# Two-layer SSD and MLA step in split fp32: norms of a series issued at once or a unit later, weights scaled on ScalarE, five PSUM banks at the scan's end

## Chip, cores and metric

One core of a Trainium2 chip runs the whole kernel. The metric is the device time of one execution in microseconds; lower is better. Engines are named as in the profile: PE (TensorE, with PEld for its weight loads), DVE (VectorE), ACT (ScalarE), POOL (GpSimd) and SP (SyncE, which here only issues DMAs).

## The reference

One inference step of a trunk of two layers over a prompt of 1024 tokens and a sample of 32 tokens, width 1024, all in fp32. Layer 0 mixes tokens by a Mamba-2 scan, layer 1 by latent attention, and each layer ends with a gated product of per-layer embeddings (`ple`). Cut to what matters here:

```python
def ple(h, p, up_w, norm_w, gate_w):
    g = sigmoid(rmsnorm(h, norm_w) @ gate_w)
    return (p @ up_w) * g
# each layer
hn = rmsnorm(h, ln_w[i]);  h = h + mixer(hn);  h = h + ple(h, p[i], ...)
# the mixer of layer 1
q_a, kv_a, k_r, gate = split(hn @ in_w, [384, 640, 672])
q      = (rmsnorm(q_a) @ q_b_w).reshape(T, 16, 96)
q_nope = rmsnorm(q[..., :64]);  q_rope = apply_rope(rmsnorm(q[..., 64:]), cos, sin)
lat    = rmsnorm(kv_a);         k_rope = apply_rope(rmsnorm(k_r), cos, sin)
kv     = (lat @ kv_b_w).reshape(T, 16, 128);  k_nope = rmsnorm(kv[..., :64]);  v = kv[..., 64:]
o      = chunk_causal_attention(q_nope, q_rope, k_nope, k_rope, v) * silu(gate)
out    = o @ out_w
```

The sample attends over a cache of 1024 past latents as well. Outputs are both hidden streams, the conv and scan states, and the new latents and rotary keys.

## The kernel before

Activations lie transposed: 128 features on the partitions, tokens along the free dimension. Prompt and sample are put together as 1056 tokens in two halves of 528. A product in fp32 is made of three products in the faster fp32r form: activation and weight are split into a high part (rounded to fp32r) and a low part (the rest), and `gemm` (line 245 is its matmul) adds up wh·ah, wh·al and wl·ah over the blocks k of 128 features. `load_weight` gets one weight block: a DMA on SP into `wraw` (two buffers), where a scale is given the multiply by it (one gain per input feature, so one number per partition and k), the copy to `wh` on ACT (L204) and the difference `wl` on POOL (L205). A block of 128 outputs over 8 k's on one half of 528 tokens is 48 matmuls of 264 columns; here it is called a product, and its result a pair of banks `pg` or `psi`, of which there are three.

The phases, with their stretch of the profiled execution in us:

- 0 to 781, `phase_ssd`: 8 groups of the scan. At the last group's end the products p @ up_w of layer 0 (`up_product`, results `upe`, stored to `u_d`) run while `finish` normalises the last group.
- 781 to 973, `phase_out`, the output product `pso` of layer 0.
- 973 to 1069, `phase_ple`: for m in 0 to 7 and two halves, a gate product `pg`, then t = pg·r (DVE, L806), tanh (ACT, L188), u·(1 + tanh) (DVE, L189), plus the residual `hr` that POOL adds up (DVE, L810). Then `emit` stores the new h to DRAM, splits it into `yhl` (ACT L259, DVE L260), squares it (ACT L702) and adds the square to `acc` (POOL L703). The weights gateW are scaled by the gain of the norm; the norm's r is one factor per token, made by `norm_r`: a matmul n of the squares with ones (L710), ln and exp.
- 1069 to 1247, `phase_mla_in`: with the scaled weights miW and krW two latent blocks, the rotary key, three blocks of q_a and eight gate blocks, each on two halves (`mblock`). r1[hf], the norm of the layer's input, is made at the first product of its half, directly behind that product's matmuls.
- 1247 to 1398, `phase_sample`: the attention of 32 tokens, interleaved with up products of layer 1 (`pup`) and with the first steps of the prompt, `Prompt.prep(0)` and `rope_block(0)`.
- 1398 to 1790, `phase_prompt`: 8 pairs of heads; `values` makes the products `psv` from the value weights vW, `fill` puts operands into `qk`, `row_max` the scores s (L1343) for the maxima, `head` the transposed scores `st` and the output o.
- 1790 to 1889 and 1889 to 1985: `phase_out` and `phase_ple` of layer 1.

`Prompt.prep` and `rope_block` are generators: each step makes a product for a group of heads, issues the norm of the product before it (`norm_now`, matmul `hn`, L936) and puts its own into `self.norms`; the last norm of a series follows when the generator is resumed after its last step. `rope_block` then swaps halves of the rotary rows by eight small DMAs on SP (L1211, L1212), loads cosines and sines (L1217, L1218) and combines them.

Within a phase the order of instructions on each engine is not the order of the code: a scheduler with a simulated timeline (`schedule_with_timeline_sim=True`) sets it when the program is built, by its own estimates, and each engine then runs its list in order. So an edit can shift instructions that it doesn't touch.

Of the kernel before, what the change touches and what calls it, by code (L numbers as in the profile page):

```python
# [10 lines left out]
F32 = mybir.dt.float32  # L11
F32R = mybir.dt.float32r
AF = mybir.ActivationFunctionType
ALU = mybir.AluOpType
# [3 lines left out]
P = 128  # L18
# [154 lines left out]
def bc_last(ap, n):  # L173
    return ap.unsqueeze(len(ap.shape)).to_broadcast(list(ap.shape) + [n])
# [17 lines left out]
def load_weight(c, src, nk, m, scale=None, eng_h=None, wp=None, wr=None):  # L192
    nc = c.nc
    wp = wp or c.wp
    raw = (wr or wp).tile([P, nk, m], F32, tag="wraw", name="wraw")
    nc.sync.dma_start(raw, src)
    if scale is not None:
        nc.gpsimd.tensor_tensor(raw, raw, bc_last(scale, m), op=ALU.mult)
    wh = wp.tile([P, nk, m], F32R, tag="wh", name="wh", bufs=c.whb)
    wl = wp.tile([P, nk, m], F32R, tag="wl", name="wl", bufs=c.whb)  # L200
    if eng_h:
        eng_h.tensor_copy(wh, raw)
    else:
        nc.scalar.activation(wh, raw, AF.Copy)  # L204
    nc.gpsimd.tensor_tensor(wl, raw, wh.bitcast(F32), op=ALU.subtract)  # L205
    return wh, wl


def load_stacked(c, src, nk, m, scale=None, eng_h=None):

    nc = c.nc
    raw = c.wp.tile([P, nk, m], F32, tag="wraw", name="wraw")
    nc.sync.dma_start(raw, src)
    if scale is not None:
        nc.gpsimd.tensor_tensor(raw, raw, bc_last(scale, m), op=ALU.mult)
    w = c.wp.tile([P, nk, 2 * m], F32R, tag="wh", name="whl", bufs=c.whb)
    wh, wl = w[:, :, :m], w[:, :, m:]
    if eng_h:
        eng_h.tensor_copy(wh, raw)
    else:  # L220
        nc.scalar.activation(wh, raw, AF.Copy)
    nc.gpsimd.tensor_tensor(wl, raw, wh.bitcast(F32), op=ALU.subtract)
    return w
# [39 lines left out]
def pvc(c, name, i=0, n=1, rows=P):  # L263
    o, _ = PV[name]
    return c.pv[:rows, o + i : o + i + n]


def up_product(c, i, piece, raw, tiles, ps_tile, evac, nb=1):

    nc, I = c.nc, c.I  # L270
    o, n = piece
    acts = []
    for k in range(2):
        x = raw()[:, :n]
        nc.sync.dma_start(x, I[f"pT{i}"][:, k, o : o + n])
        h, l = tiles()[:, :n], tiles()[:, :n]
        split(c, h, l, x)
        acts.append((h, l))
    yield
    na = -(-n // 512)  # L280
    w_ = n // na
    for m in range(8):
        b = m % nb
        if b == 0:
            ws = load_weight(c, I[f"upW{i}"][m // 4][:, 2 * (m % 4) : 2 * (m % 4 + nb)], 2 * nb, P)
        w = [x[:, 2 * b : 2 * b + 2] for x in ws]
        u = evac()
        for a in range(na):
            ps = ps_tile()
            gemm(c, ps[:, :w_], w, acts, slice(w_ * a, w_ * a + w_))  # L290
            if nb > 1 and a % 2:
                nc.vector.tensor_copy(u[:, w_ * a : w_ * a + w_], ps[:, :w_])
            else:
                nc.scalar.activation(u[:, w_ * a : w_ * a + w_], ps[:, :w_], AF.Copy)
        c.store(c.u_d[i][m][:, o : o + n], u[:, :n])
        yield
# [8 lines left out]
def phase_ssd(c, ctx):  # L305
    nc, tc, I, O = c.nc, c.tc, c.I, c.O
# [3 lines left out]
    mm = es.enter_context(tc.tile_pool(name="ps_mm", bufs=3, space=bass.MemoryType.PSUM))  # L310
    pc = es.enter_context(tc.tile_pool(name="ps_c", bufs=1, space=bass.MemoryType.PSUM))
# [334 lines left out]
    for g in range(G):  # L646
        scan_group(g, Ss[g])
        if g + 1 < G:
            bc_blocks(g + 1)
        if g:  # L650
            gate(g - 1, 0, Ss[g - 1])
            gate(g - 1, 1, Ss[g - 1])
        if g + 1 < G:
            x_block(g + 1, 0)
        else:
            gate(g, 0, Ss[g])
        if g:
            finish(g - 1, Ss[g - 1])
        if g + 1 < G:
            x_block(g + 1, 1)  # L660
            if g == 0:

                for p in steps:
                    tc.add_manual_dep(p, c.product.ins.name, mybir.DependencyInfo(
                        mybir.DependencyClass.NoSync, mybir.DependencyReason.DATA), reason="late operand")
        else:
            up = up_product(c, 0, (0, T), lambda: kp.tile([P, T1], F32, tag="cx", name="upr", bufs=6),
                            lambda: kp.tile([P, 3 + T1], F32R, tag="raw", name="upx", bufs=RAWB),
                            lambda: mm.tile([P, 512], F32, tag="mm", name="mm"),
                            lambda: kp.tile([P, T1], F32, tag="cx", name="upe", bufs=6), 4)  # L670
            next(up)
            gate(g, 1, Ss[g])
            finish(g, Ss[g])
# [13 lines left out]
def gemm2(c, ps, w, acts, first=True, last=True):  # L687

    n = len(acts)
    for k in range(n):  # L690
        for a in range(2):
            gemm(c, ps[:, a, :264], [x[:, k : k + 1] for x in w], acts[k : k + 1], slice(264 * a, 264 * a + 264),
                 first=first and k == 0, last=last and k == n - 1)
# [120 lines left out]
def phase_mla_in(c, h1s, r1, tmp, yt, mt, st, latents_done):  # L814
# [3 lines left out]
    def wt(name, tag):  # L818
        return yt.tile([P, 528], F32, tag=tag, name=name, bufs=RAWY if tag == "yraw" else 2)

    def mblock(wsrc, m, evac):
        w = (load_stacked if m < P else load_weight)(c, wsrc, 8, m, scale=pvc(c, "lnw1", 0, 8))
        for hf in range(2):
            ps = mm2(c, "psi")
            if m < P:
                for a in range(2):
                    gemm_stacked(c, ps[:, a, :264], w, h1s[hf], slice(264 * a, 264 * a + 264), m)
            else:
                gemm2(c, ps, w, h1s[hf])
            if callable(r1[hf]):  # L830
                r1[hf] = r1[hf]()
            evac(hf, ps[:, :, :264])

    def latent(nblk, wofs, n, wname, done):
        raws = [[None] * nblk for _ in range(2)]
# [352 lines left out]
class Prompt:  # L1188
# [7 lines left out]
    def rope_block(self, g):  # L1196
        c, nc, I = self.c, self.c.nc, self.c.I
        w = load_weight(c, I["qrW"][g], 3, P)
        rope = c.pre.tile([P, 2, 1024], F32, tag="rope", name="rope")
        sw, fq = rope[:, 0], rope[:, 1]  # L1200
        for a in range(2):
            cols = slice(512 * a, 512 * a + 512)
            ps = c.ps.tile([P, 512], F32, tag=self.tag, name="psr", bufs=2)
            gemm(c, ps, w, self.st.qan, cols)
            self.norm_now()
            self.norms.append((fq[:, cols], head_sq(c, ps, fq[:, cols]), pvc(c, "qr"), (c.bd32, 32)))
            yield
        self.norm_now()
        for h in range(4):
            lo, hi = slice(32 * h, 32 * h + 16), slice(32 * h + 16, 32 * h + 32)  # L1210
            nc.sync.dma_start(sw[lo], fq[hi])  # L1211
            nc.sync.dma_start(sw[hi], fq[lo])  # L1212
        for a in range(2):
            cols = slice(512 * a, 512 * a + 512)
            wc = c.pre.tile([P, 512], F32, tag="hsh", name="wcos", bufs=2)
            ws = c.pre.tile([P, 512], F32, tag="hsl", name="wsin", bufs=2)
            nc.sync.dma_start(wc, I["cosT"][:, cols])  # L1217
            nc.sync.dma_start(ws, I["sinT"][:, cols])  # L1218
            nc.vector.tensor_tensor(fq[:, cols], fq[:, cols], wc, op=ALU.mult)
            nc.vector.tensor_tensor(sw[:, cols], sw[:, cols], ws, op=ALU.mult)  # L1220
            nc.vector.tensor_tensor(fq[:, cols], fq[:, cols], sw[:, cols], op=ALU.add)
        h, l = sw.bitcast(F32R), fq.bitcast(F32R)
        nc.scalar.activation(h, fq, AF.Copy)
        nc.vector.tensor_tensor(l, fq, sw, op=ALU.subtract)
        self.rope = rope.bitcast(F32R)

    def prep(self, p):

        c, I = self.c, self.c.I
        self.x[p] = out = []  # L1230
        for wsrc, nk, acts, wn in ((I["qnW"][p], 3, self.st.qan, "qn"), (I["kW"][p], 2, self.st.latp, "kn")):
            w = load_weight(c, wsrc, nk, P)
            for a in range(2):
                ps = c.ps.tile([P, 512], F32, tag=self.tag, name="psqk", bufs=2)
                gemm(c, ps, w, acts, slice(512 * a, 512 * a + 512))
                x = c.pre.tile([P, 512], F32, tag="hx", name="hx", bufs=5)
                self.norm_now()
                self.norms.append((x, head_sq(c, ps, x), pvc(c, wn), (c.bd64, 64)))
                out.append(x)
                yield  # L1240
        self.norm_now()

    def norm_now(self):

# [366 lines left out]
```

## Time and profile before

| | before |
|---|---|
| median of 3 runs | 1989.59 us (1989.28 to 1992.05) |
| the profiled execution | 1990.86 us, span 1989.1 us |
| granted TensorE clock, mean | 0.990 |
| PE busy | 1922.0 us (97%), 12763 matmuls |
| DVE, ACT, POOL busy | 1217.8, 1064.9, 996.0 us |
| DMA | 204.26 MB, mean 103 GB/s |

The span runs from the first to the last instruction of the profiled execution; the device time holds 1.8 us more. Busy times overlap between engines. A row of waits reads: engine, its operation and line, what it waited for; total us, times, longest. A row of the timeline reads: start, duration, engine, line, operation, output<-inputs, and in brackets the idle time just ahead on that engine with what ended it. SPq is the queue of SP, where DMAs are issued.

### The profile page before, as it was taken

What the parts mean: (1) busy time and instruction counts of PE and PEld (TensorE: products, weight loads), DVE (VectorE), ACT (ScalarE), POOL (GpSimd) and SP (SyncE); (2) the same over time, 40 slices, a digit from 0 to 9 for tenths busy, and PEclk for the clock granted to TensorE, in tenths of its full rate; (3) what the DMA queues carried; (4) which work ended last, traced back from release to release, by engine and by line L of the source; (5) the groups of instructions that cost most, each with busy time, mean ns of one, the idle gap of its engine ahead of it and who ended that gap; (6) DMA issues with size and microseconds to landing.
All of it is one profiled execution on the core that took longest, in us unless ns stands there. A gap on an engine that the chain in (4) does not pass through costs nothing. (4 is left out here: it accounts for less than half of the span.)

```text
span 1989.1 us, 32537 instructions
## 1 busy us (share of the span) xinstructions
PE 1922.0 (97%) x12763; PEld 1768.4 (89%) x12763; DVE 1217.8 (61%) x1533; ACT 1064.9 (54%) x1990; POOL 996.0 (50%) x828
## 2 busy tenths in 40 slices
PE   8999999999999999999998999998899999999999
PEld 7998999999999998999998999677678777779999
DVE  7979684755757485452376543544677777755544
ACT  5445645455555546342434331777587878754331
POOL 5643434344442545545676452324466666635772
PEclk9999999999999999999999999999899999999999
DMA  4143442524333436563333221424412222316442
GB/s 142 54 97 83 102 105 76 105 74 96 91 79 86 102 100 246 167 201 109 97 115 118 73 73 71 153 83 127 98 47 72 68 54 66 112 38 200 124 130 72
DMA packets 110730, 204.26 MB, mean 103 GB/s; under 512 B 18224, under 2 KB 60720, under 8 KB 110448
## 3 DMA queue, kind: packets, MB, share of 16 engines
q1 hardware_dynamic: 105328, 193.04, 33.4%
q0 software_dynamic: 2944, 7.04, 1.8%
q8 instruction: 100, 1.64, 0.3%
q10 hardware_dynamic: 2304, 2.10, 0.3%
q14 instruction: 54, 0.44, 0.1%
HBM read 156.81 MB, written 38.83 MB: 98 GB/s over the span
## 5 line engine op out<-in xcount | busy, mean ns | idle before, releaser
L205 POOL TENSOR_TENSOR wl<-wraw,wh 128x1024 fp32r<-128x1024 f32 (+3 forms) x183 | 373.1, 2040 | 374.0 <-ACT wh L204 350.5
L245 PE MATMUL mm<-hh,wl 128*128 128x384 f32 (+1 forms) x1136 | 371.5, 327 | 0.0
L245 PE MATMUL mm<-hh,wh 128*128 128x384 f32 (+1 forms) x1136 | 371.1, 327 | 0.0
L245 PE MATMUL mm<-hl,wh 128*128 128x384 f32 (+1 forms) x1136 | 368.9, 325 | 0.0
L204 ACT ACTIVATE wh<-wraw 128x1024 fp32r<-128x1024 f32 (+3 forms) x181 | 157.1, 869 | 240.7 <-PE pso L245 96.5
L245 PE MATMUL pso<-yhl,wh 128*128 128x264 f32 x1536 | 282.9, 286 | 0.9 <-DVE hf L765 0.4
L245 PEld LDWEIGHTS pso<-yhl,wh 128*128 128x128 f32 x1536 | 238.9, 189 | 1.5 <-ACT yhl L259 1.0
L245 PE MATMUL pso<-yhl,wl 128*128 128x264 f32 x768 | 218.9, 285 | 3.6 <-POOL wl L205 3.6
L245 PEld LDWEIGHTS mm<-hh,wh 128*128 128x128 f32 x1136 | 213.5, 188 | 3.5 <-issue 3.2
L245 PEld LDWEIGHTS mm<-hl,wh 128*128 128x128 f32 x1136 | 213.8, 188 | 0.8 <-issue 0.2
L245 PEld LDWEIGHTS mm<-hh,wl 128*128 128x128 f32 x1136 | 213.5, 188 | 0.9 <-issue 0.2
L503 DVE SCALAR_TENSOR_TENSOR cx<-raw,pv,cx 128x1060 f32<-128x1060 f32 x96 | 144.7, 1511 | 44.0 <-ACT cx L501 43.4
L566 ACT ACTIVATE ex<-ex,tokT 128x128 f32<-128x128 f32 (+1 forms) x288 | 87.2, 380 | 136.3 <-DMA ex<-acs_d 128.5
L245 PE MATMUL psi<-yhl,wh 128*128 128x264 f32 x832 | 156.3, 289 | 1.6 <-ACT yhl L259 1.2
L1363 PE MATMUL st<-qk 128*128 128x512 f32 (+2 forms) x576 | 149.0, 370 | 4.6 <-ACT pf L1369 3.3
L245 PEld LDWEIGHTS pso<-yhl,wl 128*128 128x128 f32 x768 | 145.6, 190 | 4.6 <-POOL wl L205 4.6
L245 PE MATMUL pg<-hH,wl 128*128 128x264 f32 x512 | 145.5, 284 | 1.3 <-POOL wl L205 1.3
L245 PE MATMUL pg<-hH,wh 128*128 128x264 f32 x512 | 146.1, 285 | 0.0
L245 PE MATMUL pg<-hL,wh 128*128 128x264 f32 x512 | 145.7, 285 | 0.0
L579 POOL TENSOR_TENSOR hm<-hT,cd_all 128x256 f32<-128x256 f32 x64 | 53.6, 838 | 162.1 <-DVE hT L581 97.0
L245 PEld LDWEIGHTS psi<-yhl,wh 128*128 128x128 f32 x832 | 131.5, 192 | 2.9 <-ACT yhl L259 1.4
L1345 DVE TENSOR_REDUCE mx<-s 128x1 f32<-128x128 f32 (+2 forms) x192 | 101.8, 550 | 50.6 <-PE s L1343 49.4
(547 smaller groups left out, 4638.3 us busy)
## 6 DMA issues: line engine op xcount, KB each, us to landing
wraw<-in_inW SPq DMA_DIRECT2D x48, 512.0 KB, 3.5
ex<-acs_d SPq DMA_DIRECT2D x32, 512.0 KB, 5.5
wraw<-in_outW SPq DMA_DIRECT2D x32, 512.0 KB, 3.8
yraw<-y_d SPq DMA_DIRECT2D x32, 264.0 KB, 4.6
u<-u_d SPq DMA_DIRECT2D x32, 264.0 KB, 2.9
eb<-ea_d SPq DMA_DIRECT2D x64, 128.0 KB, 3.8
y_d<-y SPq DMA_DIRECT2D x16, 512.0 KB, 2.8
wraw<-in_gateW SPq DMA_DIRECT2D x16, 512.0 KB, 3.5
```

The lines of the kernel that those rows point to most:

```text
L204: nc.scalar.activation(wh, raw, AF.Copy)
L205: nc.gpsimd.tensor_tensor(wl, raw, wh.bitcast(F32), op=ALU.subtract)
L245: p = c.nc.tensor.matmul(ps, ww[:, k, :m], aa, start=first and k == 0 and i == 0, stop=last and k == n - 1 and i == 2)
L503: nc.vector.scalar_tensor_tensor(xh, raw[:, k : k + T1], pvc(c, "cw", 4 * b + k), xh, op0=ALU.mult, op1=ALU.add)
L566: nc.scalar.activation(e_, e_, AF.Relu, scale=-1.0, bias=tok(32)[:, i, h : h + 1])
L579: nc.gpsimd.tensor_tensor(hm.rearrange("p (h q) -> p h q", q=64), hT.rearrange("p (h q) -> p h q", q=64), bc_last(cd_all[:, hs, ch], 64), ...
L1345: nc.vector.tensor_reduce(mx[:, col : col + 1], ps[:, : (w if b else 128)], axis=AX.X, op=ALU.max)
L1363: nc.tensor.matmul(ps[:, :n], a_[:, ks], b_[:, q], start=t == 0, stop=t == 2)
```

## The change

Four edits.

- `load_weight` and `load_stacked` scale a weight by 8 ACTIVATEs on ACT, one for each k with the gain as the per-partition scale, in place of one multiply on POOL. It concerns 16 gateW, 13 miW and the krW.
- In `mblock` of `phase_mla_in`, the norm r1 of a half and the evacuation of its first product are put into a list and issued behind the next product.
- The up products of layer 0 cycle over five PSUM banks (three of `mm`, and two that the scan used, `trx` and `trb`) instead of three.
- In `rope_block` and `prep` the norm of the last product of a series is issued right behind that product, ahead of the last `yield`, and not when the generator is resumed.

```diff
@@ load_weight, and the same in load_stacked
     if scale is not None:
-        nc.gpsimd.tensor_tensor(raw, raw, bc_last(scale, m), op=ALU.mult)
+        for k in range(nk):
+            nc.scalar.activation(raw[:, k], raw[:, k], AF.Identity, scale=scale[:, k : k + 1])
@@ phase_ssd, the up products
+            banks = itertools.cycle(((mm, "mm"), (mm, "mm"), (pc, "trx"), (mm, "mm"), (pc, "trb")))
+
+            def up_bank():
+                pool, tag = next(banks)
+                return pool.tile([P, 512], F32, tag=tag, name="mm")
...
-                            lambda: mm.tile([P, 512], F32, tag="mm", name="mm"),
+                            up_bank,
@@ phase_mla_in, mblock
+    late = []
...
                 gemm2(c, ps, w, h1s[hf])
+            if late:
+                late.pop()()
+
+            def rest(hf=hf, ps=ps):
+                if callable(r1[hf]):
+                    r1[hf] = r1[hf]()
+                evac(hf, ps[:, :, :264])
+
             if callable(r1[hf]):
-                r1[hf] = r1[hf]()
-            evac(hf, ps[:, :, :264])
+                late.append(rest)
+            else:
+                rest()
@@ Prompt.rope_block
             self.norms.append((fq[:, cols], head_sq(c, ps, fq[:, cols]), pvc(c, "qr"), (c.bd32, 32)))
+            if a:
+                self.norm_now()
             yield
-        self.norm_now()
@@ Prompt.prep
-        for wsrc, nk, acts, wn in ((I["qnW"][p], 3, self.st.qan, "qn"), (I["kW"][p], 2, self.st.latp, "kn")):
+        for b, (wsrc, nk, acts, wn) in enumerate(((I["qnW"][p], 3, self.st.qan, "qn"), (I["kW"][p], 2, self.st.latp, "kn"))):
...
                 out.append(x)
+                if a and b:
+                    self.norm_now()
                 yield
-        self.norm_now()
```

Lines of the changed kernel are 1 to 22 higher than those of before. The program has 240 more instructions on ACT and 30 fewer on POOL; matmuls, DMAs and table loads are as many. Three places show what moves.

ACT in the first layer's gate products, one block (two halves). Before: square of the second half of a block, tanh and yhl of the next, its square, the weight's wh, and on.

```order
L188 ACTIVATE t_10794<-t_10794 128x528
L259 ACTIVATE yhl<-u 128x528
L702 ACTIVATE sq<-u 128x528
L204 ACTIVATE wh<-wraw 128x1024
L188 ACTIVATE t_10860<-t_10860 128x528
L259 ACTIVATE yhl<-u 128x528
L702 ACTIVATE sq<-u 128x528
```

In the change:

```order
L188 ACTIVATE t_10836<-t_10836 128x528
L199 ACTIVATE wraw<-wraw,pv 128x128 x8
L261 ACTIVATE yhl<-u 128x528
L710 ACTIVATE sq<-u 128x528
L205 ACTIVATE wh<-wraw 128x1024
L188 ACTIVATE t_10902<-t_10902 128x528
L261 ACTIVATE yhl<-u 128x528
```

The eight scalings of the next weight stand between tanh and yhl of a block's first half, ahead of the wh of the same weight.

SP at the start of the prompt. Before, the last of the rotary DMAs, two stores of up products, and the loads of the first value weights:

```order
L1211 DMA rope<-rope 16x1024
L1212 DMA rope<-rope 16x1024
L170 DMA u_d_110<-upe 128x352
L170 DMA u_d_111<-upe 128x352
L196 DMA wraw<-in_vW 128x512
L196 DMA wraw<-in_qnW 128x384
```

In the change:

```order
L170 DMA u_d_108<-upe 128x352
L170 DMA u_d_109<-upe 128x352
L196 DMA wraw<-in_vW 128x512
L196 DMA wraw<-in_qnW 128x384
L170 DMA u_d_110<-upe 128x352
L170 DMA u_d_111<-upe 128x352
```

The eight rotary DMAs stand some 40 rows further up, and the value weights are ahead of the last two stores.

PE at the same place. Before, the last up product, the end of the sample's attention (`pu`, `pz`) and the first value products:

```order
L245 MATMUL pup<-upx,wl 128x352
L1132 MATMUL pu<-cst,un 128x128 x2
L1139 MATMUL pz<-ut,wv 128x64 x4
L1315 MATMUL psv<-wh,lpH_11161 128x256
L1315 MATMUL psv<-wh,lpL_11162 128x256
```

In the change:

```order
L1365 MATMUL s_14737<-qk_14683 128x448
L247 MATMUL pup<-upx,wl 128x352
L247 MATMUL pup<-upx,wh 128x352 x2
L247 MATMUL pup<-upx,wl 128x352
L1385 MATMUL st<-qk_14683 128x512
L1365 MATMUL s_14740<-qk_14683 128x512
L1337 MATMUL psv<-wh,lpH_11217 128x256
L1337 MATMUL psv<-wh,lpL_11218 128x256
```

Scores s and st of the first heads now stand among the last up products, ahead of the first psv.

More of the change, by code (lines that the diff above doesn't have):

```diff
@@ L214, in load_stacked @@
     if scale is not None:
-        nc.gpsimd.tensor_tensor(raw, raw, bc_last(scale, m), op=ALU.mult)
+        for k in range(nk):
+            nc.scalar.activation(raw[:, k], raw[:, k], AF.Identity, scale=scale[:, k : k + 1])
     w = c.wp.tile([P, nk, 2 * m], F32R, tag="wh", name="whl", bufs=c.whb)
```

## Prediction

> **What bounds the kernel now.** I read the page's head and busy line first, then the clock, then the span cut into stretches.
>
> ```profile
> PE 1922.0 (97%) x12763; PEld 1768.4 (89%) x12763; DVE 1217.8 (61%) x1533; ACT 1064.9 (54%) x1990; POOL 996.0 (50%) x828
> ```
>
> ```profile
> core 0: 1989.1 us, clock 0.990
> ```
>
> PE is busy 1922.0 of 1989.1 us, so TensorE is the bound and 67.1 us of its time stand idle. The clock of 0.990 is the second loss, since a matmul at half the clock takes twice as long: about 0.010 × 1989 = 20 us of work-time are lost to it. The change removes no matmul, so it can only win from these 87 us, and can lose by making new idle time. The stretches show where they lie (columns: stretch, length, busy time of PE, weight loads, DVE, ACT, POOL, granted clock, DMA share, GB/s).
>
> ```profile
> 742.00:800.00 58.00, 53.62 (x365) 52.21 (x364) 34.21 (x33) 38.15 (x62) 29.71 (x17) 1.00 0.68 239
> 1028.00:1110.00 82.00, 74.91 (x559) 72.52 (x559) 48.98 (x45) 31.07 (x48) 52.47 (x31) 0.94 0.30 95
> 1110.00:1247.00 137.00, 137.00 (x1106) 134.70 (x1105) 64.44 (x69) 42.49 (x61) 54.13 (x30) 1.00 0.25 81
> 1376.00:1432.00 56.00, 43.90 (x190) 33.59 (x189) 33.28 (x57) 34.22 (x69) 30.97 (x43) 0.83 0.57 129
> 1432.00:1790.00 358.00, 346.67 (x1677) 276.47 (x1676) 256.51 (x413) 284.40 (x574) 210.25 (x202) 0.99 0.24 64
> ```
>
> Three stretches that the change touches lose time: the scan's end (58.00 − 53.62 = 4.4 us idle), the passage from the gate products to the latent products (7.1 us idle, and 0.06 × 82 = 4.9 us of clock), and the start of the prompt's attention (12.1 us idle and 0.17 × 56 = 9.5 us of clock). Together 38 us: the ceiling, apart from the 11.3 us that lie scattered over the prompt. What PE waited for there, from the waits of each stretch in turn:
>
> ```profile
> PE mm L245 <- ACT upe L294: 2.3, 2, 2.1
> PE mm L245 <- DVE upe L292: 2.0, 2, 1.7
> ...
> PE n L710 <- POOL acc L703: 3.1, 2, 2.8
> PE pg L245 <- POOL wl L205: 1.3, 1, 1.3
> PE psi L245 <- ACT yhl L259: 1.2, 1, 1.2
> PE psi L245 <- POOL wl L205: 1.1, 1, 1.1
> ...
> PE psv L1315 <- ACT wh L204: 3.0, 1, 3.0
> PE psv L1315 <- POOL wl L205: 0.7, 1, 0.7
> ```
>
> **Part 1, five banks at the scan's end.** Nothing is added; the up products get two more banks of PSUM. Their waits on evacuations (2.3 + 2.0 us, all but the whole 4.4 us idle) should go. But the stage ends with the normalisation of the last group, which needs ACT, DVE and POOL and not PE: PE that runs ahead meets it earlier. Bounds 0 (all given back) and 4.4; I take 2.5, a little over the middle, because the evacuations of the up products stand in front of that normalisation on ACT and no longer hold it up.
>
> **Part 2, weights scaled on ScalarE.** 29 weights lose one POOL multiply of 128x1024 and one (the rotary key's) a small one; each gets 8 ACTIVATEs of 128x128 with a per-partition scale. That form is not in the trace; the nearest is the ACTIVATE with a per-partition bias of the same shape.
>
> ```profile
> L566 ACT ACTIVATE ex<-ex,tokT x288: 304/387/404, 130.3 to 731.1; 128x128 f32<-128x128 f32 x128, 32x32 f32<-32x32 f32 x16
> ```
>
> The rows of the place that counts, from the timeline (start, duration, engine, line, operation, and the idle time ahead with what ended it):
>
> ```profile
> 1033.03 0.69 DVE L806 TENSOR_TENSOR t<-pg,r 128x528 f32<-128x528 f32 x1
> 1035.31 2.39 DVE L810 SCALAR_TENSOR_TENSOR u<-u,hr 128x528 f32<-128x528 f32 x1
> 1046.48 0.70 DVE L806 TENSOR_TENSOR t<-pg,r 128x528 f32<-128x528 f32 x1
> 1048.76 0.71 DVE L810 SCALAR_TENSOR_TENSOR u<-u,hr 128x528 f32<-128x528 f32 x1
> 1031.52 0.43 SPq L196 DMA_DIRECT2D wraw<-in_gateW  x1
> 1035.23 1.90 POOL L198 TENSOR_TENSOR wraw<-wraw,pv 128x1024 f32<-128x1024 f32 x1 [0.93 <-DMA wraw<-in_gateW]
> 1037.73 0.65 ACT L259 ACTIVATE yhl<-u 128x528 fp32r<-128x528 f32 x1 [3.27 <-DVE u L810]
> 1038.82 1.05 ACT L204 ACTIVATE wh<-wraw 128x1024 fp32r<-128x1024 f32 x1
> ```
>
> Of one the duration is 0.304 to 0.387 us; overlapped, 8 take 2.4 us, end to end 3.1. So ACT gains 29 × 2.4 = 70 us of 924 free and POOL loses 29 × 1.9 = 55 us: neither sum matters, only the place. In the stretch 1110 to 1247 and in the last layer's gate PE does not wait (137.00 of 137.00) and a weight is loaded a product ahead: cost nothing; if that cover is gone, each weight costs at most 2.4 − 1.9 = 0.5 us more.
>
> The place that counts is the first layer's gate products. There the evacuation is a chain: DVE t, ACT tanh, DVE u, DVE u, ACT yhl, DVE yhl, then the next t. From the t at 1033.03 to the one at 1046.48, two halves of one block later, are 13.45 us, while PE needs 2 × 5.83 = 11.7 us (a product of 48 matmuls, below). So the chain is slower than PE by 1.8 us per block; PE lives on its lead and then stalls (the waits on wl and yhl above). What makes the chain slow is DVE beside POOL: the same u takes 0.71 us at 1048.76 and 2.39 at 1035.31, while POOL scales a weight from 1035.23 to 1037.13. Without POOL's multiply that u would end 1.7 us sooner, at 1036.0, and the period would be 11.8. But the 8 ACTIVATEs now stand on ACT between tanh and yhl, and can't start before the weight has landed, which POOL's start shows as 1035.23: they end at 1035.23 + 2.4 = 1037.7. yhl behind them starts at 1037.7, as before (1037.73), and wh at 1038.8, as before (1038.82). The period stays 13.45: a wait on a neighbour becomes a wait in the queue, gain nothing per block.
>
> At the start of the phase it costs. The changed order has the first such 8 between the first tanh and the first yhl, and the norm of the second half (ln and exp of r) behind them.
>
> ```profile
> 980.33 0.33 SPq L196 DMA_DIRECT2D wraw<-in_gateW  x1
> 983.00 0.65 ACT L259 ACTIVATE yhl<-u 128x528 fp32r<-128x528 f32 x1 [2.78 <-DVE u L810]
> 989.01 0.65 ACT L183 ACTIVATE r<-r 128x528 f32<-128x528 f32 x1
> ```
>
> The weight issued at 980.33 lands 3.7 us later (1035.23 − 1031.52), at 984.0; 8 of them end at 986.4, and yhl goes from 983.00 to 986.4: 3.4 us later, and the exp of 989.01 with it. Where the buffer comes free later than at 980.33, it is later by as much, up to the 2.4 us of a subtraction on POOL; I take 5.5. At the last block the small weight's 8 add 8 × 0.3 = 2.4 us ahead of a tanh, less the POOL time before. The chain thus ends 5.5 to 9 us later, central 8.
>
> **Part 3, norms one unit later.** In the latent products, the norm matmul of the second half (n) stood right behind the first product and now stands one product later, so the wait for POOL's acc is covered.
>
> ```profile
> 1085.05 0.71 DVE L260 TENSOR_TENSOR yhl<-u,yhl 128x528 fp32r<-128x528 f32 x1 [0.71 <-ACT yhl L259]
> 1089.87 2.13 PE L710 MATMUL n<-acc,ones 128*128 128x264 f32 x4 [2.83 <-POOL acc L703]
> 1099.68 0.71 DVE L840 TENSOR_TENSOR lraw<-psi,r 128x528 f32<-128x528 f32 x1 [5.53 <-PE psi L245]
> 1105.51 0.71 DVE L840 TENSOR_TENSOR lraw<-psi,r 128x528 f32<-128x528 f32 x1 [5.12 <-PE psi L245]
> ```
>
> From the last yhl (ends 1085.76) to the end of the fourth product (1105.5) were 19.7 us. After it there remain at least the six matmuls that read it (6 × 5.83/48 = 0.7), two norms of 1.1 (the row's 2.13 halved, since it ran, as I read the stretch's 0.94, at half the clock) and two products of 5.83: 14.6 us, if no half clock follows. Gain 5.1. Parts 2 and 3 meet here: PE waits for that yhl, 8 us later. Sum −2.9; another 0.6 for the latent norm moved into the next products, which its users see later: **−3.5 us**, bounds −12 (8 at 0.387 in each of 7 blocks: 7 × 0.7 = 5 more, and one more window of half clock, 3.4) and +10 (period 11.8, all of the stretch's 12.0 us but 2).
>
> **Part 4, the prompt's norms at once.** The last norm of a series was issued when the generator was resumed, and is now issued with its product; so the rotary rows of the first heads, their eight DMAs on SP and the two loads of cosines and sines move ahead of dozens of SP rows, and the value weights no longer stand behind them. SP's waits and its rows, with those of ACT and PE that follow from them:
>
> ```profile
> SPq L1217 <- PE hn L936: 3.2, 1, 3.2
> SPq L1211 <- DVE rope L939: 2.4, 1, 2.4
> ```
>
> ```profile
> 1384.24 4.49 SPq L170 DMA_DIRECT2D u_d<-upe  x2
> 1391.20 0.52 SPq L1211 DMA_DIRECT2D rope<-rope  x1
> 1397.62 0.38 SPq L196 DMA_DIRECT2D wraw<-in_vW  x1
> 1400.92 1.04 ACT L204 ACTIVATE wh<-wraw 128x512 fp32r<-128x512 f32 x2 [3.48 <-DMA wraw<-in_vW]
> 1401.98 0.42 PE L1315 MATMUL psv<-wh,lpL 128*128 128x256 f32 x1
> 1410.12 0.28 PE L1315 MATMUL psv<-wh,lpL 128*128 128x256 f32 x1
> 1410.71 0.40 PE L1343 MATMUL s<-qk 128*128 128x256 f32 x2
> ```
>
> Before, SP issued the value weights (1397.62) after eight rotary DMAs (the first at 1391.20) and two stores; ACT's wh came 3.3 us later, and PE's psv waited 3.0 and 0.7 us for it. After, they stand right behind the pair of stores of 1384.24 to 1388.7: wh about 1392, so 3.7 us of PE's idle time go. The same psv takes 0.42 at 1401.98 and 0.28 at 1410.12: a lower clock after the gap, for most of the 8.1 us between; at half the clock 4.1 of them are lost work. The score products s for the row maxima, which first ran at 1410.71, are now interleaved with the sample's tail and may fill its other gaps: of the 21.6 us of the stretch 13.8 are still unnamed, and I give this 1.2. 3.7 + 4.1 + 1.2 = **9**, bounds 2 (the gap alone closes partly and the clock still drops elsewhere) and 14 (two thirds of the 21.6 us).
>
> Here a rule differs. The Trainium skill ("TensorE: Matmul & The Clock Gate", Part 1, What's actually happening) says that the clock halves after at least one idle window of some 3.4 us. By it a gap of 3.0 us leaves the clock alone, closing it wins no clock back, part 4 gives an estimated 4.9 and the sum is 4.4. The row behind the gap speaks for 9.
>
> Over the rest of the prompt the order is shuffled by the same edit: 11.3 us idle lie there, some may go or come; 0, bounds −4 and +4. The passage to the output product has a shorter wait: +0.5.
>
> **Sum.** 2.5 − 3.5 + 9 + 0 + 0.5 = 8.5 us of the profiled execution's 1990.86 (span 1989.1 and 1.8 around it): 1982.4. The median of the runs is 1989.59, 1.3 lower; I predict 1982. A measurement of this kernel can tell about 0.2%, 4 us.
>
> **Rivals.** *The chain is freed*, the better side: the weight lands before the second u ends, the 8 ACTIVATEs hide, the period falls to 11.8 and PE is the bound; parts 2 and 3 give +8 instead of −3.5: 20 in all, 1971. For it: the stretching of DVE beside POOL is real. Against: 1035.23, when the weight is there, is only 0.1 us ahead of that u's start.
>
> *ACT's queue costs more*: each of the 8 takes 0.387 and PE loses a window of clock, −12 instead of −3.5: 2.5 − 12 + 9 + 0.5 = 0, 1991, no change. The Trainium skill ("ScalarE: Activation LUTs", Rules for kernel authors) advises VectorE and not ScalarE for multiplying; no run here shows it yet, and this is the case in which it would be right.
>
> *The prompt gives it back*: the value weights come earlier, but the shuffled prompt stalls elsewhere; part 4 nets 1: 1990.
>
> *The clock is not won back*: it stays at half around the prompt's start, since other gaps remain there (13.8 us of loss are unnamed). 9 − 4.1 = 4.9, in all 4.4: 1986.5, on the edge of what can be told.
>
> *Slower, scores block PE*: s stands on PE ahead of the first psv. If its rotary rows come as late as before, PE stands from the end of the tail (1400.9, less psv's wait of 3.0 and about 0.7 from wh to PE: 1398.6) until 1410.7, 12.1 us, with 4.1 of clock behind it: 16.2 in place of 7.8, −8.4 instead of +9. 2.5 − 3.5 − 8.4 + 0.5 = −8.9: 2000. It decides from about 8 us of standing on (8 + 4.1 − 7.8 = 4.3 lost). Against it: their DMAs now stand some 40 rows of SP earlier. For it: PE and SP each take their rows in order, and waits of 3.2 and 2.4 us were on these very rows.
>
> **Chances.** Forecast 0.44 (its own range 1977 to 1987), freed chain 0.12, ACT's queue 0.15, prompt gives back 0.10, clock 0.05, scores block 0.14. Faster by over 0.2%: forecast and freed chain, 0.56. Slower by over 0.2%: the blocked scores and a third of ACT's queue, 0.19. The rest, 0.25, is the same. The range starts at the freed chain, 1971, and takes in the worse half of ACT's queue and part of the blocked scores up to 1996; beyond it about 2 in 10 are left.
>
> **What would show it.** Right: no wait of mm on upe at 760 to 772; ACT L199 in eights of about 0.3 us with a DMA wait ahead; t to t 13 to 13.5 us per block; n without a 2.8 us wait; psv's wait on wh gone, and the clock full around it. Wrong: a period near 11.8 (freed), waits on yhl or wl spread over more blocks than the last (queue), s waiting for a DMA of qk (scores), or st, ph and pl waits in the prompt over 11.3 us together (given back).

## The result: slower, and the profile after

Timed beside the kernel before on the same chips (15 runs of each), the changed kernel takes 1997.27 us (median) against 1992.05 us, a ratio of 1.0029 with a 95% interval of 1.0018 to 1.0041. I had forecast 1982 and a gain; the time lies just above the range of 1971 to 1996. The profiled execution after took 1993.89 us with a span of 1991.8; the one before 1990.86 and 1989.1.

Page of the changed kernel, busy times, and behind it the same stretches as before:

```profile
PE 1915.7 (96%) x12763; PEld 1767.0 (89%) x12763; DVE 1194.2 (60%) x1533; ACT 1133.2 (57%) x2230; POOL 930.1 (47%) x798
```

```profile
742.00:800.00 58.00, 55.37 (x383) 54.40 (x382) 35.61 (x33) 38.98 (x64) 28.68 (x16) 1.00 0.70 243
1028.00:1110.00 82.00, 76.42 (x584) 74.33 (x584) 45.15 (x49) 47.10 (x103) 39.42 (x25) 0.96 0.33 105
1376.00:1432.00 56.00, 44.89 (x214) 37.52 (x215) 25.65 (x47) 28.26 (x63) 24.55 (x31) 0.88 0.52 117
1432.00:1790.00 358.00, 338.40 (x1619) 267.52 (x1617) 254.69 (x403) 282.14 (x568) 209.38 (x202) 0.99 0.24 64
```

ACT has 68 us more and POOL 66 us less, where I had worked out 70 and 55. PE's idle time fell a little at the scan's end, in the gate and latent products, and at the prompt's start. But from 1432 to 1790 it rose from 11.3 to 19.6 us. Because fixed windows mix work that has moved, I cut the traces at fixed points of the work instead. The times are worked out from the first and last matmuls of each product, each from one profiled execution ("pss" are the scores of the sample, "the last o" the last output product of the prompt's attention):

| us | before | after |
|---|---|---|
| first up product to end of output product pso | 221.1 | 220.9 |
| to end of latent, q_a and gate products psi | 274.8 | 271.2 |
| to the last score pss of the sample | 129.5 | 129.1 |
| to the last o of the prompt | 413.7 | 423.3 |
| the rest, to the last gate product pg | 193.5 | 191.0 |

All of the loss, 9.6 us, lies between the sample's last score and the prompt's last output: 3.5 us of it up to the last output po of the sample (17.9 us before, 21.4 after), 6.1 us behind that, in the prompt. The windows of that stretch, before and after:

```profile
1377.23:1790.94 413.71, 390.28 (x1864) 309.75 (x1862) 289.44 (x468) 318.08 (x642) 241.20 (x244) 0.97 0.28 72
```

```profile
1372.88:1796.17 423.29, 391.06 (x1871) 310.99 (x1871) 284.54 (x460) 315.66 (x640) 239.58 (x245) 0.98 0.28 71
```

PE's waits in it, first before:

```profile
PE st L1363 <- ACT pf L1369: 3.3, 8, 0.6
PE s L1343 <- DVE mx L1345: 1.4, 4, 0.5
```

and after:

```profile
PE s L1365 <- DVE mx L1367: 5.8, 9, 1.7
PE st L1385 <- ACT pf L1391: 5.8, 6, 3.2
PE s L1365 <- ACT qk L1307: 3.9, 1, 3.9
PE o L1409 <- DVE pl L1406: 3.0, 3, 1.8
PE pup L247 <- ACT upe L296: 2.8, 1, 2.8
```

PE's busy time is the same within 0.8 us; 8.8 of the 9.6 us are idle time. psv's wait of 3.0 us on wh has shrunk to 0.3, and five others took its place. Two of them lie in the sample's tail: pup on upe (2.8) and s on ACT's qk (3.9, the longest single wait). In the timeline (POOL, SP, ACT, PE):

```profile
1372.52 1.13 POOL L1306 DMA_DIRECT2D qk<-in_qka  x2
1373.62 1.09 POOL L1322 DMA_DIRECT2D qk<-rope  x2
...
1373.33 0.46 SPq L1295 DMA_DIRECT2D krt<-kr_d  x1
1377.45 9.96 SPq L170 DMA_DIRECT2D u_d<-upe  x2
1396.11 0.83 SPq L170 DMA_DIRECT2D u_d<-upe  x2
1397.03 0.41 SPq L196 DMA_DIRECT2D wraw<-in_vW  x1
...
1372.24 4.39 ACT L1321 ACTIVATE qk<-hx 64x512 fp32r<-64x512 f32 x8
1384.28 2.13 ACT L1307 ACTIVATE qk<-krt 32x1024 fp32r<-32x1024 f32 x2 [5.25 <-DMA krt<-kr_d]
1386.63 0.44 ACT L296 ACTIVATE upe<-pup 128x352 f32<-128x352 f32 x1
...
1377.48 0.59 PE L247 MATMUL pup<-upx,wh 128*128 128x352 f32 x2 [2.79 <-ACT upe L296]
1385.39 0.79 PE L1365 MATMUL s<-qk 128*128 128x256 f32 x2 [3.88 <-ACT qk L1307]
```

The landing time of krt, before and after:

```profile
DMA to landing us min/median/max: 3.8/3.8/3.8
```

```profile
DMA to landing us min/median/max: 10.9/10.9/10.9
```

The rotary key rows krt (512 KB) are issued at 1373.33, just behind four operand loads on POOL (two of 512 KB, two of 256 KB), and land 10.9 us later, against 3.8 us before. ACT's copy waits for them, the score s at the head of PE's queue waits for the copy, and the up products behind s wait with it. The wait of 2.8 us just before comes from the same fill: eight copies of qk from hx hold ACT from 1372.24 to 1376.63, and the copy upe that frees the bank of pup stands behind them. SP's queue stands twice. From 1377.45 to 1387.4 the second of two stores waits for the upe of 1386.63; its product was ready at 1379.2, but the upe stood on ACT behind the copies of krt. The next two stores wait until 1396.1 for products whose matmuls stand behind s and behind the sample's outputs po on PE; they were done at 1395.1 and 1396.0. Behind them the value weights are issued at 1397.03, where before it was 1397.62: they came 0.6 us earlier, where some 9 had been meant.

### The profile page after: what moved, and what is told of

It reads as the page before. It is cut to its first block, busy times and chain, and to the rows that moved or that the text cites. A ratio compares the mean times of both kernels' runs of the same rounds, so it can differ in the third digit from the quotient of the medians.

```text
span 1991.8 us, 32748 instructions
## 1 busy us (share of the span) xinstructions
PE 1915.7 (96%) x12763; PEld 1767.0 (89%) x12763; DVE 1194.2 (60%) x1533; ACT 1133.2 (57%) x2230; POOL 930.1 (47%) x798
```

## The experiments

Each kernel was timed beside the kernel before in five rounds. Ratios have 95% intervals. "Tail" is the time from the sample's last pss to its last po, "end" that from the last pss to the prompt's last o; before they are 17.9 and 413.7.

### The parts undone, in the changed kernel

Part 4 undone (both hunks of `rope_block` and `prep` put back):

> The changed kernel with part 4 undone (last norm of a series issued on resuming, as before); parts 1 to 3 stay. Theory A (part 4 is the loss: the scores stand in PE's queue and wait for operands that five DMAs bring at once, and the prompt is shuffled): the scan's end, the gate products and the latent products keep their gain of about 3.9 us at the end of the latent products (1243.8 against 1247.7), and the rest is as before: span 1985 to 1987, ratio to before 0.998 to 0.999. Rival B (the loss comes from weights on ScalarE, or from any reshuffling of the prompt): span 1989 to 1993, the prompt from 1432 on again with 17 to 20 us of idle PE.

Ratio 1.0006 (0.9996 to 1.0016). The tail is 16.2 us without a wait of s, and krt lands in 3.9 us, so the tail's loss is of part 4; but the end takes 420.6 us, and the gain that theory A expected does not come. Both theories are half right: something else than part 4 also makes the prompt longer.

Part 2 undone (`nc.gpsimd.tensor_tensor(raw, raw, bc_last(scale, m), ...)` put back):

> The changed kernel with part 2 undone (weights scaled on POOL again). My prediction's theory (the period of a gate block is held either by DVE beside POOL or by the ACTIVATEs in ACT's queue, the same 13.2 to 13.5 us): the period stays, the last yhl comes within 1 us of 1087.3, span within 2 us of 1991.8. Rival (ACT's queue costs): the last yhl comes 2 to 4 us sooner, PE's wait of 3.5 us on yhl goes, span 1987 to 1989. Second rival (POOL's relief is worth something): the last yhl comes 1.5 us or more later, span 1994 or more.

Ratio 1.0036 (1.0025 to 1.0047), span 1996.3, the latent and gate products 269.9 us against 271.2 after. By its span the second rival would be right; by the place it isn't. This execution was 4.7 us later already at the end of pso, ahead of most of the scaling, and s waited 6.2 us for krt. Counted from the end of pso, the last yhl comes 1.3 us sooner than in the changed kernel (113.4 against 114.7 us): the price of part 2 there in this pair. Over all sixteen kernels of this text it comes at 113.3 us on average without ScalarE scaling and at 114.1 with it, so 0.9 us.

### Parts alone, in the kernel before

Part 4 alone:

> The kernel before with part 4 alone. Theory A: the sample's tail and the prompt's start lose 3 to 4 us and the prompt some 5 more: span 1995 to 1999, ratio 1.003 to 1.005, with a wait of PE's s on ACT's qk copy of 3 to 5 us near 1385. Rival B: span 1987 to 1991, no such wait.

Ratio 1.0095 (1.0082 to 1.0108), span 2009.9: worse than the whole change, tail 23.0, end 433.8, krt landing in 11.8 us, s waiting 5.1. Theory A, and more than it expected.

Part 3 alone (`late` in `mblock`), and parts 2 and 3:

> The kernel before with part 3 alone (norm of the second half and its evacuation one product later). PE's order in the sample and the prompt stays word for word that of before. Theory C (the last stretches are lost by the order that the scheduler makes, parts 2 and 3 by themselves gain): the latent and gate products take 174 us instead of 178.9, the prompt is as before: span 1984 to 1985.5, ratio 0.997 to 0.9985. Rival D (the prompt's 7 us come whatever is changed ahead of it, by the time at which it starts): gain eaten, span 1989 to 1992.

> The kernel before with parts 2 and 3, order of PE in the sample and the prompt as before. By the difference of the runs without and with ScalarE scaling so far (174.0 against 176.0 us of latent and gate products) part 2 costs 2 us: span 1986 to 1988, 1.5 to 3 above part 3 alone. Rival: part 2 costs nothing or wins, span within 1 us of part 3 alone.

Ratios 0.9984 (0.9970 to 0.9998) and 0.9992 (0.9980 to 1.0004). The gate and latent products take 270.2 and 270.5 us instead of 274.8, the ends 413.6 and 413.4: as before. Part 3 gains 4.6 us there, part 2 costs 0.3. For part 3 this is theory C, though its span of 1988.8 lies above the 1984 to 1985.5 that were expected; for part 2 it is well below the 2 us expected. The two spans (1988.8 and 1982.9) differ by more than 0.3 since the stretches ahead of and behind it each vary by some 2 us between executions. All the kernels together say the same of this stretch: 273.3 to 275.9 us without parts 2 and 3 (five kernels), 269.8 to 270.9 with part 3 (five), 270.2 to 271.2 with both (six). By the averages part 3 gains 4.9 us and part 2 costs 0.5.

Part 1 alone (five banks), and one half of part 4, the one in `prep`:

> The kernel before with part 1 alone (five banks). The scheduler gives PE another order in the prompt, though no line of it is touched. Theory C: up products end up to 2 us sooner, the prompt from the first psv to the last o takes 395 to 399 us instead of 389.3: span 1992 to 1996, ratio 1.001 to 1.003. Rival E (the prompt's loss comes of parts 2 or 3 or of chance between profiles): prompt within 2 us of 389.3, span 1986 to 1988.

> The kernel before with the half of part 4 in prep alone: the rotary rows stay where they were, no score moves into the sample's tail, but PE's order in the prompt is another. Theory A (the score that stands in PE's queue is the loss of part 4): no loss in the tail, prompt within 3 us of 389.3, span 1987 to 1992. Theory C (the order of the prompt as well): tail as before (17 to 18 us from the last pss to the last po), prompt 394 us or more, span 1993 to 1999.

Ratios 1.0040 (1.0026 to 1.0054) and 1.0045 (1.0032 to 1.0058). Ends 423.5 and 422.2 us, with no score in the tail of either and krt landing in 3.8 and 4.4 us. Theory C holds for both in the prompt: no line of it is touched by part 1, yet it loses 10 us there. In the tail the second missed its expectation: 20.3 us and not 17 to 18, with no wait on operands, PE busy 1.5 us longer and a granted clock of 0.66 in it where before had 0.81. Waits of PE over the end with the banks alone:

```profile
PE s L1349 <- DVE mx L1351: 8.8, 8, 3.5
PE o L1393 <- DVE pl L1390: 3.7, 7, 1.3
```

The scheduler lays the instructions of the prompt out anew, and PE's scores now stand where the maxima on DVE (mx), which free their banks, are not yet done: 8.8 us of waits where there were 1.4. Of the 9.8 us in all, 5.4 are idle time of PE, and 4.4 are longer busy time at a clock of 0.96 instead of 0.97.

The other half of part 4, the one in `rope_block`:

> The kernel before with the half of part 4 in rope_block alone: scores move into the sample's tail as in the changed kernel. Theory A: the tail from the last pss to the last po takes 21 to 23.5 us instead of 17.9, with a wait of s of 3.5 to 6.5 us on the operand rows; prompt order changed, span 1997 to 2006, ratio 1.003 to 1.008. Rival (both halves are needed for the loss in the tail): tail 17 to 18.5, no such wait.

Ratio 0.9979 (0.9965 to 0.9992), span 1984.6. Both theories failed: scores do move into the tail, and it gets shorter, 15.4 us, with psv 0.2 us behind the last pz (before 3.0). Its timeline (SP, POOL) tells why, with the landing time of krt behind it:

```profile
1374.33 0.40 SPq L1274 DMA_DIRECT2D krt<-kr_d  x1
1385.48 3.91 SPq L170 DMA_DIRECT2D u_d<-upe  x2
1390.91 0.33 SPq L196 DMA_DIRECT2D wraw<-in_vW  x1
...
1379.11 1.13 POOL L1285 DMA_DIRECT2D qk<-in_qka  x2
1380.21 1.09 POOL L1301 DMA_DIRECT2D qk<-rope  x2
```

```profile
DMA to landing us min/median/max: 4.1/4.1/4.1
```

krt goes out 4.8 us ahead of POOL's four loads, and lands in 4.1 us. The value weights leave at 1390.91, 6.7 us earlier than before: this is the gain that the prediction had meant, though smaller than its 9 us: the end is 410.7 us, 3.0 less than before. Only with the `prep` half added are the operands ready sooner, and POOL's loads run beside krt.

### The collision of loads

krt issued from POOL, ahead of the four loads (`nc.gpsimd.dma_start(krt, ...)` for `nc.sync`), in the changed kernel:

> The changed kernel, but the rotary key rows (krt) are loaded by POOL's queue ahead of its four big operand DMAs, instead of by SP just after them. Theory A1 (all five DMAs share the bandwidth, the last operand to land decides): krt lands in 4 to 6 us instead of 10.9, but the operand rows land as late as before; the wait of s (3.9 us) falls by 1 us at most; span within 1.5 us of 1991.8. Theory A2 (krt alone is late): the wait of s falls below 1 us and the half clock behind it goes: span 1986 to 1988.

Ratio 1.0047 (1.0032 to 1.0061), span 1995.1. krt lands in 7.2 us, later than the 4 to 6 expected, and the wait moves on. The longest wait of PE at this place, and the landing time of krt:

```profile
PE s L1365 <- DMA qk<-rope: 4.6, 1, 4.6
```

```profile
DMA to landing us min/median/max: 7.2/7.2/7.2
```

So A1, with a span 1.8 us beyond its bound: whichever of the five goes first, the last decides, and s needs all of them. How full the DMA engines are while krt is under way, before and after (the last two columns are their busy share and GB/s):

```profile
1373.10:1377.80 4.70, 4.53 (x24) 3.50 (x23) 1.53 (x3) 1.11 (x3) 0.59 (x1) 1.00 0.56 172
```

```profile
1373.30:1384.30 11.00, 5.42 (x28) 4.76 (x26) 4.21 (x12) 5.70 (x16) 10.07 (x22) 0.84 1.13 233
```

After, their share is twice that of before (1.13 against 0.56) over the whole time that krt takes.

Half of the constant operand rows, which is zero, written by a memset on POOL:

```diff
-            nc.gpsimd.dma_start(qk["t"][par][gp], I["qka"].rearrange("a p n -> p a n"))
+            nc.gpsimd.dma_start(qk["t"][par][gp, 0:2], I["qka"][0:2].rearrange("a p n -> p a n"))
+            nc.gpsimd.memset(qk["t"][par][gp, 2:4].bitcast(F32), 0.0)
```

> The changed kernel, with the half of the constant operand rows that is zero written by POOL's memset and not loaded: 0.5 MB less of the 2.1 MB that are in flight together. Theory A1 (shared bandwidth): krt lands in 7 to 9.5 us instead of 10.9, the wait of s falls from 3.9 to 1 to 2.5 us. Rival (the load is late for its own length or its place in a queue): 10 us or more, wait 3.5 us or more. The prompt's order changes again, so the whole: 1988 to 1997.

Ratio 1.0009 (0.9996 to 1.0021), against 1.0029 for the change itself. krt lands in 6.8 us and s waits 0.7, less than expected; the tail is 16.2. PE's order is another again, with an end of 416.8 us, so the ratio holds more than the loads. The memsets between the loads also spread them (5.7 us from the first issue to the end of the last instead of 2.2), so bytes and timing are not told apart here. That the loads collide is shown by this run and the rotary half alone: with 0.5 MB less and more space between the loads, or with krt 4.8 us ahead of the others, the wait all but goes.

### The value weights by themselves

Part 3, and the load of the first value weights (`load_weight` with a queue of its own) from POOL, or from ACT:

> Part 3 alone, and the load of the first value weights issued from POOL's queue instead of SP's, so that it is not behind stores and rotary DMAs. My prediction's term for the prompt's start: psv's wait of 3.2 us on wh falls below 1 us, the half clock behind it goes, 4 to 8 us less up to the end of the first psv. Theory C (order): the scheduler also gives PE another order later in the prompt; from the first psv's end to the last o 382 to 388 us instead of 377.5. Together span 1985 to 1992, ratio 0.998 to 1.001. Rival (only the start counts): later prompt 377 to 379, span 1978 to 1982, ratio 0.994 to 0.996.

> As the kernel with the value load on POOL's queue, but from ACT's queue: the same start of the prompt, another order of PE after it. If the prompt's time is a matter of the order drawn: from the first psv's end to the last o between 377 and 390 us, and different by more than 2 us from the kernel with the load on POOL. Start: psv's wait on wh below 1 us. Span 1980 to 1992.

Ratios 1.0000 (0.9989 to 1.0010) and 0.9969 (0.9957 to 0.9981). The gap between the last pz and the first psv goes from 3.2 us to nothing in both; a wait of 1.8 and 2.4 us (on DVE's os, which frees the bank) comes inside it. From the sample's last pss to the end of the first eight psv products they take 34.1 and 33.6 us, where part 3 alone has 36.2. From there to the last o the two take 383.2 and 381.0 us, where the order of before has 377.5, and they differ by 2.2 between them, as an order drawn anew would make them: the early load gains 2.1 and 2.6 us at the start, less than the 4 to 8 expected, and 5.7 and 3.5 are lost to the new order.

### What wins, put together

Part 3 with the rotary half of part 4; and the same with ScalarE scaling, which is the change without part 1 and without the `prep` half:

> The kernel before with part 3 and the rotary half of part 4. PE's order in the sample and prompt is that of the rotary half alone. If the loss comes from the combination of the two halves of part 4 and from part 1, the gains of part 3 (about 5 us in the gate and latent products) and of the rotary half (4 us up to the first psv) add: span 1978 to 1982, ratio 0.994 to 0.997, tail 15 to 16 us, krt lands in under 5 us. Rival (any two of the edits together collide): ratio 0.998 or more.

> The changed kernel without part 1 and without the prep half of part 4, so with ScalarE scaling, late norm and the rotary half. If part 2 costs nothing, as the kernel with parts 2 and 3 had it: span within 1.5 us of the kernel without ScalarE scaling, ratio 0.994 to 0.997. If part 2 costs: 2 us more, ratio 0.995 to 0.998.

Ratios 0.9929 (0.9914 to 0.9944) and 0.9941 (0.9928 to 0.9955): the gains add, both kernels are faster than the kernel before and the changed one, and ScalarE scaling is worth nothing, or 0.1% against it (the intervals overlap). Medians 1979.7 and 1980.5 us. The ratio is better than the product of the two parts' own (0.9984 × 0.9979 = 0.9963); why it is more than a sum is not shown. Page and, behind it, windows of the first:

```profile
PE 1911.4 (97%) x12763; PEld 1764.4 (89%) x12763; DVE 1213.0 (61%) x1533; ACT 1065.7 (54%) x1990; POOL 993.2 (50%) x828
```

```profile
1028.00:1110.00 82.00, 76.64 (x593) 74.32 (x592) 52.84 (x50) 34.80 (x54) 53.27 (x32) 0.98 0.32 106
1376.00:1432.00 56.00, 50.22 (x247) 40.19 (x248) 33.76 (x57) 37.16 (x81) 33.06 (x43) 0.94 0.46 104
```

At the prompt's start PE is idle 5.8 us instead of 12.1, and the clock is at 0.94 instead of 0.83.

### One table for the order

PE's list of the sample and the prompt, compared instruction by instruction between the kernels, falls into groups that are word for word alike. The time from the last pss to the last o, by group:

| PE's order in sample and prompt | kernels | us |
|---|---|---|
| as before | before, part 3, parts 2 and 3 | 413.7, 413.6, 413.4 |
| with the five banks | banks alone, change without part 4 | 423.5, 420.6 |
| of the changed kernel | after, with scaling on POOL | 423.3, 424.9 |
| of the rotary half | alone, with part 3, with parts 2 and 3 | 410.7, 408.9, 409.1 |
| six more, one kernel each | value load on ACT, half the operand bytes, value load on POOL, `prep` half, krt first, part 4 alone | 414.7, 416.8, 417.4, 422.2, 423.6, 433.8 |

Within a group the spread is 0.3 to 2.9 us, whatever else differs; between groups it is up to 16, and 25 with the single ones. Nor do the parts add: part 4 alone costs this stretch 20.1 us, the banks alone 9.8, and the change with both 9.6. So the time of this stretch goes with the order that the scheduler draws. The waits go with it too: PE's scores wait for mx for 1.2 to 1.4 us in the three kernels of the first group, 8.8 and 7.0 in the second, 5.8 and 5.9 in the third and 2.8 in all three of the fourth. Parts 2 and 3, which leave the order alone, leave time and waits alone. That the order is the cause, and not the banks or norms that came with it, rests on these likenesses: no kernel with five banks and the old order was run, and none with a new order and no other change.

## Why the prediction was wrong, step by step

- *The sum by its places*, in the profiled pair: the scan's end and output product −0.2 us (forecast −2.5), gate and latent products −3.6 (forecast +3.5), last pss to last o +9.6 (forecast −9), the last products −2.5 (forecast −0.5). So two terms failed: part 4 together with the prompt by 18.6 us, and parts 2 and 3, which came out 7.1 us better. That the total of the pair is only 11.5 us off is luck: the two errors offset each other.
- *What bounds the kernel* held: in the stretch that lost, PE's busy time moved by 0.8 of 9.6 us, and the loss was waits.
- *Part 1, +2.5*: mis-sized at its place and blind beyond it. Over the kernels with it the up products take 27.7 to 29.2 us, without it 28.5 to 29.8; the output product behind them then takes 193 to 196 us instead of 190 to 192 (PE waits 1.2 to 1.9 us for yhl). Together 222.1 us on average over the six kernels with it, 220.6 over the ten without: 1.5 lost, just below the bound of 0. The waits on upe fell only from 4.3 to 2.6 us. The 10 us in the prompt were no term of this part at all.
- *Part 2*: the steps held closely. Of the 8 ACTIVATEs, of yhl behind them and of the t of two blocks:

```profile
1035.18 2.45 ACT L199 ACTIVATE wraw<-wraw,pv 128x128 f32<-128x128 f32 x8 [1.11 <-DMA wraw<-in_gateW]
1037.53 0.63 ACT L261 ACTIVATE yhl<-u 128x528 fp32r<-128x528 f32 x1
...
1032.63 0.69 DVE L814 TENSOR_TENSOR t<-pg,r 128x528 f32<-128x528 f32 x1
1045.80 0.70 DVE L814 TENSOR_TENSOR t<-pg,r 128x528 f32<-128x528 f32 x1
1086.56 0.71 DVE L262 TENSOR_TENSOR yhl<-u,yhl 128x528 fp32r<-128x528 f32 x1 [0.71 <-ACT yhl L261]
```

2.45 us where I had 2.4; yhl at 1037.5 where I had 1037.7; a period of 13.2 us where I had 13.45 (the blocks vary from 12 to 14.5). So the rival of a freed chain is out: the wait moved from DVE beside POOL into ACT's queue. What was mis-sized is the delay of the chain, 8 us: the last yhl comes 1.5 us later than before (1.9 counted from the end of pso). POOL, without its multiply, freed the buffer sooner: the third weight was issued at 977.86, not 980.33, so that the first yhl came at 983.76, 0.8 us later than before and not 3.4. The Trainium skill ("ScalarE: Activation LUTs", Rules for kernel authors) advises VectorE and not ScalarE for multiplying. These runs don't test it, since the multiply left POOL and none ran on VectorE; against POOL, ScalarE costs 0.5 us in this stretch by the averages above, and no difference that the ratios can tell.
- *Part 3, 5.1*: right, 4.6 us by part 3 alone. With the delay of part 2 cut down, the two come to +3.6 and not to −3.5.
- *Part 4, +9*: here the sum broke. The step "they stand right behind the pair of stores of 1384.24 to 1388.7: wh about 1392" took the issue time of the stores from the trace of before. In the changed order the two stores ahead of the value weights wait for up products that PE finishes only behind s and po, so they left at 1396.1 and not at 1384.24 to 1388.7; and the two stores before them had already held the queue from 1377.45 to 1387.4, since ACT's copy upe stood behind the copies of krt. What it cost is the rival *scores block PE*, at 0.14: right in mechanism (s waits at the head of PE's queue, 3.9 us, with a granted clock of 0.50 from 1384.9 to 1391.5), but not for late rotary rows; the operands were early, all of them at once, and the standing was half of the 8 us from which that rival decides. The rotary half alone then gave what the step had promised, the value weights 6.7 us earlier and psv without a wait on wh, but 3.0 us of time and not 9; ratio 0.9979.
- *Rest of the prompt, 0 ± 4*: the term that decided. I had the changed list before me and priced its shuffling as noise around nothing. What these runs show instead: of the nine other orders, eight are slower than before's, by 1.0 us (less than the spread within a group) to 20.1, and one is faster. Before's order was a good draw, and a new one is likelier to be worse. What in a list makes it slow is known only by its waits (mx, pf, pl), not by a rule, and stays open.
- *The clock*: the Trainium skill ("TensorE: Matmul & The Clock Gate", Part 1) has the clock halve after at least one idle window of about 3.4 us. The traces show half the clock behind shorter gaps, as the prediction took it. Before, PE has two gaps of 1.10 and 1.25 us, up to 1379.97 and 1382.85; the six microseconds that hold most of them, and the four after:

```profile
1376.00:1382.00 6.00, 4.32 (x26) 3.33 (x24) 4.06 (x10) 5.28 (x11) 4.71 (x16) 1.00 0.58 141
1382.00:1386.00 4.00, 3.15 (x11) 2.67 (x12) 0.69 (x3) 3.92 (x11) 3.99 (x6) 0.58 1.22 232
```

PE was busy 4.3 of the 6 us ahead, and the clock fell all the same. Where part 3 closes the gap of 2.83 us ahead of n, the clock of its stretch rises from 0.94 to 0.98 (part 3 alone, 1028 to 1110).

## What to carry to other kernels

Where a scheduler lays out the order, price an edit by two things apart: what it does at its place, and what the new layout does elsewhere; compare the lists first, and keep the edits that leave the far list alone (parts 2 and 3 here) apart from those that redraw it. Making something ready earlier helps only if what it then triggers doesn't run into something else: here the operands of a fill, ready sooner, sent five loads of 2 MB together, and the score behind them needed all five. And undo a bundle by halves: the change as a whole lost 0.29%, and without one part and a half of another it gains 0.6%.

## What the runs showed of the hardware

A load of 512 KB that is issued 4.5 us or more ahead of the other loads of its fill lands in 3.6 to 4.4 us, and in 10.9 to 11.8 us beside four others of 1.5 MB, all issued within 2.3 us. Giving it the first place shortens it to 7.2 us and leaves the score as late: 12.8 us after the first of the five issues, against 12.9. A DVE operation on 128x528 that takes 0.71 us by itself takes 2.4 to 2.8 beside a POOL operation on 128x1024; taking POOL's multiply away gained nothing here, since ACT, which took it over, stands in the same chain. The granted clock fell to 0.58 around two gaps of PE of 1.10 and 1.25 us.
